# Moving the weights' tiles to multiples of 256 bytes, and 512-wide activation sets in a pool of their own, in a two-layer decoder trunk

## The chip, the cores and the metric

The kernel runs on one core of a Trainium2 chip. The metric is device time in microseconds (us), the median of three runs. A core has five engines with their own instruction queues: TensorE (PE, with its weight loads listed apart as PEld), VectorE (DVE), ScalarE (ACT), GpSimd (POOL) and SyncE (SP), which here only issues DMAs. All work on tiles in the on-chip memory SBUF, which has 128 partitions. In this document a tile's **place** is the byte at which it begins within its partition.

## The reference, cut to what matters

A sequence of 512 tokens, with 16 learned meta tokens ahead of it (528 columns in all), passes two layers of width 1024. Both layers end in the same kind of MLP:

```
mix = even_mixer(hn, ...) if layer % 2 == 0 else odd_mixer(hn, ...)
h = h + mix
h = h + sq_relu_mlp(rmsnorm(h, norm_mlp_g[layer]), mlp_w1[layer], mlp_w2[layer])

def sq_relu_mlp(h, w1, w2):
    return jnp.square(jax.nn.relu(h @ w1)) @ w2        # 1024 -> 4096 -> 1024
```

Layer 0 mixes by a retention and a convolution (weights `w_in`, `w_out`), layer 1 by stick-breaking attention (`w_qkv`, `w_o`). The meta tokens are dropped at the end, so the last products of layer 1 (its output projection and its MLP) are needed for 512 columns alone, while everything before works on 528. All of it is float32.

## The kernel before, in words

Features lie on the partitions, tokens along them. The weights come in 219 blocks of 128 output columns (`raw`, 4 KB in each partition), in the order of use. Each block is split into a high and a low float32r part, `whi` and `wlo`, of the same size. Pool `wp` holds two `raw`, three `whi` and three `wlo`; one part of 128 input features is 512 bytes of each.

Activations are split in the same manner into sets of eight pairs (`new_set`): for each 128 input features a high tile and a low tile. `products` forms, for one such part k, three products, each on the array with the part's 128x128 weights loaded for it: high weights by high activations (the rows `...h,whi` of a profile), high by low (`...l,whi`), low by high (`...h,wlo`). The weights are the operand that is loaded, the activations the operand that streams. Where there are 528 columns, each product is two of 264, one for each half. A call of `gemm` runs the eight parts, 48 products of 264 columns or 24 of 512. The loads of weights are instructions of their own; each is begun while the product before it streams.

By line L282 go 8448 products: 6528 of 264 columns (layer 0, and layer 1's keys and values) and 1920 of 512 (layer 1's queries 192, its output projection 192, its MLP 1536).

The MLP goes by four quarters of the 4096 hidden features. A quarter's hidden activations are a set `hid`; quarters 0 and 2 take one group of places, 1 and 3 another. In layer 1, quarters 0 and 2 take the places in pool `act` (tag "B") where the attention's output lay before, 1 and 3 those of pool `mlp1` (tag "C"). The input set of that MLP, `x3`, is in pool `actA`.

Pools are laid one behind the other, so a tile that grows moves all that lies behind it. Sets are made of tiles T = 528 columns wide, 2112 bytes, which is 64 more than a multiple of 256; eight pairs run through the remainders 0, 64, 128, 192. What a set's tile begins with is thus the same in every other part: even k has its high tile at remainder 0 and its low one at 64, odd k at 128 and 192. The second half of 264 columns lies 1056 bytes on, 32 more than a multiple of 256.

Layer 0's mixer and the attention have an order written out by hand (`Between`, `manual_schedule`), the MLPs follow the order of the code.

Of the kernel before, what the change touches and what calls it, by code (L numbers as in the profile page):

```python
# [17 lines left out]
P = 128  # L18
# [12 lines left out]
# Layer 0. What a tap of the convolution counts against DVE's share of a step, and how much of the share may pile up  # L31
TAP, CAP = 0.70, 1.5
# per head, the steps from one chunk of the retention to the next
WAIT = (2, 5, 3, 1)
# steps before the two sums of the layer norm
LW = (3, 1)
# per head, the steps from a chunk of the next head's retention to the turning back of this one
AGE = (2, 3, 1, 1)
# the block of w_in after which the input carries the tokens' norm
RN = 6  # L40
# products of zeros at the start; parts by which the second block lags; the part after which the norm is taken
WARM, LAG, RK = 10, 2, 0
# the pieces in which a block of the weights is split during layer 0's mixer and the attention
CUTS = 4
# Layer 1, in steps from the start of a head's work: scores of a block of queries (Z), turning of a
# block of keys (T), products with the values (V), end of a head (E), turning of the meta keys (M)
ZS, TS, VS = (0, 1, 1, 3), (10, 10, 10, 13), (16, 18)
ES, MS = (23, 30), 20
# steps before the norm of the keys, its Newton step, a pair's heads, the turning of the values
# [11 lines left out]
# columns of the parameter block  # L61
# [10 lines left out]
# columns of the constant block: what depends on shapes alone  # L72
# [15 lines left out]
# pairs of heads whose part of w_o is added while the last heads are still at work  # L88
# [3 lines left out]
def unit_order():  # L92
    """The 128-column blocks of the weights, in the order in which they are used."""
    units = []
    for j in range(NK):
        units += [("w_in", 0, 4096 + j * P), ("w_in", 0, 3072 + j * P)]
    for h in range(RH + 1):
        if h < RH:
            units += [("w_in", 0, 512 + h * P), ("w_in", 0, h * P)]
            units += [("w_in", 0, 1024 + h * 256 + e * P) for e in range(2)]  # L100
        if h > 0:
            units += [("w_in", 0, 2048 + (h - 1) * 256 + e * P) for e in range(2)]
    for part in range(2):
        units += [("w_out", part * D, m * P) for m in range(NK)]
    units += mlp_units(0)
    for p in range(8):
        units += [("w_qkv", 0, p * P), ("w_qkv", 0, D + p * P), ("w_qkv", 0, 2 * D + p * P)]
    units += [("w_oa", 0, m * P) for m in range(NK)]
    units += [("w_ob", KA * P, m * P) for m in range(0, NK, NK // (NK - KA))]
    units += mlp_units(1)  # L110
    return units
# [17 lines left out]
def trunk(ctx, tc, xT, wts, par, con, out):  # L129
# [14 lines left out]
    # the convolution's input: DVE's second operand from SBUF would shut out Pool, and the reverse  # L144
# [29 lines left out]
    def prepare(n=1, now=1):  # L174
        """The next block of the weights in two parts, the first `now` of n pieces at once."""
# [44 lines left out]
    class Between:  # L220
        """Work that goes between the products of a block, a step at a time.

        A chain tells after each step what it took of TensorE and of DVE; the filling
        takes what is left of DVE's share, and None ends it for this step."""
# [27 lines left out]
        def turn(self, n=1):  # L252
            """For the use of the spare banks of PSUM, n steps after the last."""
            while self.idle < n:
                yield None
            self.idle = 0
# [4 lines left out]
        def chain_up(self):  # L261
            """Everything but the filling, to its end."""
# [21 lines left out]
    def gemm(what, x, n, at=NK, each=None):  # L284
        """One 128-column block of x @ w, features on partitions: 3 float32r products."""
# [19 lines left out]
    def new_set(pl, tag, name):  # L305
        return [
            (pl.tile([P, T], F32R, tag=f"{tag}h{k}", name=f"{name}h{k}"),
             pl.tile([P, T], F32R, tag=f"{tag}l{k}", name=f"{name}l{k}"))
            for k in range(NK)
        ]  # L310
# [11 lines left out]
    class Sum:  # L322
# [12 lines left out]
        def total(self, dst, scale, bias=0.0, banks=None):  # L335
            """dst = scale * sum + bias on every partition."""
# [25 lines left out]
    def rsqrt(dst, xv, shape, name, pl=None, tag="rs"):  # L362
        """dst = xv ** -0.5: the table's value and a Newton step."""
# [5 lines left out]
    def rstd(sums, name, scaled=False, pl=None, tag="rb", banks=None):  # L369
        n = sums.n  # L370
        xv = sp.tile([P, T], F32, tag="xv", name=f"{name}xv", bufs=1)
# [8 lines left out]
    def residual(what, x, n, norm=None, xset=None, name="", keep=True):  # L380
        """h += x @ w, and what the next norm and product need of h."""
# [26 lines left out]
    oz = cp.tile([P, 2], F32, name="oz")  # L408
# [4 lines left out]
    # TensorE's clock opens after some work: products of zeros until the data is there  # L413
# [18 lines left out]
    # the first two blocks follow the arrival of h, the second LAG parts behind  # L432
# [37 lines left out]
    # convolution: ACT starts two sums, DVE adds the other taps to them in turn  # L470
# [36 lines left out]
    def conv_all():  # L507
# [8 lines left out]
        # layer norm  # L516
# [16 lines left out]
        xv = sp.tile([P, T], F32, tag="xv", name="lnxv", bufs=1)  # L533
# [51 lines left out]
    def normal(k):  # L585
        """The normalised input, in places that are free yet."""
# [9 lines left out]
    def renorm(k):  # L596
        """After block RN the input carries the tokens' norm."""
        nc.scalar.copy(setA[k][0], ys[k])
        if k:
            renorm_low(k - 1)  # L600
# [10 lines left out]
    # the third block, in the banks that are free yet  # L611
# [50 lines left out]
    def retention(hd, kr, qr, vt):  # L662
# [7 lines left out]
        for c in range(len(CH) + 1):  # L670
            yield from between.turn()
            if c < len(CH):
                c0, n = CH[c]
                cs = slice(c0, c0 + n)
                # tokens on partitions
# [5 lines left out]
                # scores, decayed  # L681
# [31 lines left out]
        # group norm  # L713
# [26 lines left out]
    def gated(hd, e, g):  # L740
        """Back to features on partitions, gate."""
# [48 lines left out]
    def mlp(layer, x, s, n, mine, after):  # L790
        rb = None
        with tc.tile_pool(name=f"mlp{layer}", bufs=1, reuse_waits="tile") as pl, tc.tile_pool(name=f"mlpt{layer}", bufs=2, reuse_waits="tile") as pt2:
            hid = {}
            res = None
            for which, c in MLP_STEPS:
                if which == 1:
                    hid[c] = new_set(*(mine if c % 2 == 0 else (pl, "C")), f"hid{layer}{c}")
# [39 lines left out]
    # products of what the nearer keys left; column 0 stays 1  # L837
    Eb = [ap1.tile([P, T - P * q], F32, name=f"E{q}") for q in range(NQ)]
    # meta keys of a pair of heads: 16 columns each at 0 and 64, again at 32 and 96, zero between
# [5 lines left out]
    # their transpose, per head the high part on 32 partitions and the low part on the next 32  # L845
# [37 lines left out]
    def queries(p):  # L883
        """A pair of heads in two parts, and what the scales of the scores need, tokens on partitions."""
# [32 lines left out]
    def keys(p, qxv):  # L917
        """An RMS-normalised pair of heads in two parts; the token's own norm cancels."""
# [12 lines left out]
        def chain():  # L931
# [27 lines left out]
            # the two parts of a head on the two halves of the partitions  # L959
# [11 lines left out]
    def values(p):  # L971
        """Tokens on partitions, high and low part side by side."""
# [33 lines left out]
    def attend(p, vs):  # L1006
# [8 lines left out]
        def Z(a, q):  # L1015
            """Stick-breaking weights of a head and a block of queries, keys nearest first."""
# [31 lines left out]
        def turn(a, kb):  # L1048
            """Keys on partitions."""
# [41 lines left out]
    def token_norm():  # L1091
        """The token norm, features and tokens on partitions."""
# [10 lines left out]
    def done(k):  # L1103
        """The place of setE's k-th part goes to the attention's output."""
# [21 lines left out]
    setF = new_set(actA, "A", "x3")  # L1126
# [18 lines left out]
    mlp(1, setF, s, SEQ, (act, "B"), after1)  # L1145
# [77 lines left out]
```

## Time and profile before

| | |
|---|---|
| median of three runs | 1414.18 us (1413.68 to 1415.06) |
| span of the profiled execution | 1411.5 us |
| TensorE busy | 1391.4 us, 99% of the span |
| VectorE busy | 877.5 us, 62% |
| ScalarE busy | 606.6 us, 43% |
| GpSimd busy | 357.8 us, 25% |
| DMA, share of 16 engines | 30.3% |

The span runs from the first to the last instruction; the profile gives no total for the profiled execution beside it. The timed runs are 2.2 to 3.6 us longer than this span, which is the start and end around it. A matmul's record in the profile is longer than the step from its start to the next one's, because matmuls overlap in the array and their ends are modelled; the record's length still shifts with the step.

### The profile page before, as it was taken

To read this page: it belongs to the slowest core of one execution; us is meant where nothing else is said; L and a number is where in the kernel's file an instruction comes from. 1 tells how busy PE (TensorE), PEld (TensorE's weight loads), DVE (VectorE), ACT (ScalarE), POOL (GpSimd) and SP (SyncE) were. 2 spreads that over 40 slices of the span, in tenths; PEclk is the share of its full clock that TensorE was granted. 3 is DMA by queue.
4 is the path that set the end of the run, shared out by engine and by line. 5 is a ranking of instruction groups with operands and counts; after the bars stand their busy time and mean duration, and the time that the engine had idled before them with its cause. 6 is when DMAs were issued, how large, how long until landed. Compare 5 with 4: busy or idle time off the path is not lost.

```text
span 1411.5 us, 23379 instructions
## 1 busy us (share of the span) xinstructions
PE 1391.4 (99%) x9396; PEld 1278.0 (91%) x9396; DVE 877.5 (62%) x1461; ACT 606.6 (43%) x1136; POOL 357.8 (25%) x414
## 2 busy tenths in 40 slices
PE   8999999999999999999999999998999999999998
PEld 7999999999999999999999889997878888888887
DVE  5998999966344434334345899999985433434332
ACT  6434545567443313223132677776454322323220
POOL 2656455355500000000016433335640000000000
PEclk9999999999999999999999999999999999999999
DMA  5332121123223222332233434333323332232332
GB/s 200 92 94 87 61 76 61 61 75 105 91 90 90 90 90 91 90 90 91 90 91 89 143 98 134 98 101 91 90 90 104 96 99 90 100 94 91 104 97 82
DMA packets 39643, 134.00 MB, mean 95 GB/s; under 512 B 4976, under 2 KB 5104, under 8 KB 39536
## 3 DMA queue, kind: packets, MB, share of 16 engines
q1 hardware_dynamic: 39536, 132.52, 30.3%
q8 instruction: 74, 1.21, 0.4%
q14 instruction: 33, 0.27, 0.1%
HBM read 117.69 MB, written 2.10 MB: 85 GB/s over the span
## 4 chain that ended last, share of the span: by engine, by line
PE 93%; DVE 4%; issue 1%; ACT 1%; POOL 0%; DMA 0%; POOLq 0%; SPq 0%; ACTq 0%; DVEq 0%
PE mm L282 72%; PE qk L282 11%; PE pz L1031 2%; PE po L1063 1%; PE pw L1053 1%; PE po L693 1%; DVE mT L1074 1%; PE po L697 1%; PE po L695 0%; DVE acc L489 0%; PE pk L936 0%; PE pv L679 0%; PE pt L751 0%; PE pq L899 0%; DMA h<-xT 0%
## 5 line engine op out<-in xcount | busy, mean ns | idle before, releaser
L193 ACT CAST whi<-raw 128x256 fp32r<-128x256 f32 (+1 forms) x338 | 212.0, 659 | 501.0 <-PE mm L282 461.9
L194 POOL TENSOR_TENSOR wlo<-raw,whi 128x256 fp32r<-128x256 f32 (+1 forms) x334 | 280.2, 857 | 285.6 <-ACT whi L193 136.1
L194 DVE TENSOR_TENSOR wlo<-raw,whi 128x1024 fp32r<-128x1024 f32 (+1 forms) x134 | 165.3, 1234 | 21.9 <-ACT whi L193 14.8
L385 DVE TENSOR_TENSOR h<-mm,h 128x528 f32<-128x528 f32 (+1 forms) x64 | 44.9, 701 | 214.1 <-PE mm L282 214.1
L489 DVE SCALAR_TENSOR_TENSOR acc<-cx,ptm,acc 128x526 f32<-128x526 f32 (+28 forms) x232 | 157.6, 740 | 3.5 <-ACT cx L484 3.5
L282 PE MATMUL mm<-xnh,whi 128*128 128x264 f32 x640 | 136.0, 294 | 0.0
L282 PE MATMUL mm<-xnl,whi 128*128 128x264 f32 x640 | 130.7, 286 | 2.4 <-DVE xnl L318 2.2
L282 PE MATMUL mm<-xnh,wlo 128*128 128x264 f32 x640 | 130.9, 286 | 0.0
L282 PE MATMUL mm<-x1h,whi 128*128 128x264 f32 x512 | 104.8, 286 | 0.0
L282 PE MATMUL mm<-x1h,wlo 128*128 128x264 f32 x512 | 104.3, 285 | 0.0
L282 PEld LDWEIGHTS mm<-xnh,whi 128*128 128x128 f32 x640 | 101.7, 191 | 2.8 <-issue 1.3
L282 PE MATMUL mm<-x1l,whi 128*128 128x264 f32 x512 | 103.7, 284 | 0.0
L282 PEld LDWEIGHTS mm<-xnl,whi 128*128 128x128 f32 x640 | 99.6, 190 | 3.2 <-DVE xnl L318 2.5
L282 PE MATMUL mm<-x3h,wlo 128*128 128x512 f32 x256 | 101.8, 398 | 0.0
L282 PE MATMUL mm<-x3l,whi 128*128 128x512 f32 x256 | 100.3, 392 | 0.5 <-DVE x3l L318 0.5
L282 PE MATMUL mm<-x3h,whi 128*128 128x512 f32 x256 | 100.3, 392 | 0.0
L282 PEld LDWEIGHTS mm<-xnh,wlo 128*128 128x128 f32 x640 | 100.0, 189 | 0.1
L332 POOL TENSOR_TENSOR n2s<-n2q,n2q 128x528 f32<-128x528 f32 x1 | 1.9, 1869 | 339.3 <-ACT n2q L351 339.3
L282 PE MATMUL qk<-x2h,whi 128*128 128x264 f32 (+1 forms) x320 | 82.9, 323 | 0.4 <-ACT kraw L923 0.4
L805 DVE SCALAR_TENSOR_TENSOR r<-mm,m0rb 128x528 f32<-128x528 f32 x32 | 22.7, 708 | 96.3 <-PE mm L282 96.2
L282 PEld LDWEIGHTS mm<-x1h,whi 128*128 128x128 f32 x512 | 80.2, 189 | 0.1
L282 PEld LDWEIGHTS mm<-x1h,wlo 128*128 128x128 f32 x512 | 79.8, 188 | 0.0
(400 smaller groups left out, 3343.3 us busy)
## 6 DMA issues: line engine op xcount, KB each, us to landing
raw<-wts SPq DMA_DIRECT2D x217, 512.0 KB, 3.5
Q<-qhl SPq DMA_DIRECT2D x32, 256.0 KB, 4.5
K<-khl SPq DMA_DIRECT2D x32, 132.0 KB, 3.6
h<-xT SPq DMA_DIRECT2D x8, 264.0 KB, 5.9
out<-h SPq DMA_DIRECT2D x8, 256.0 KB, 2.0
ctm<-con SPq DMA_DIRECT2D x1, 790.0 KB, 7.0
raw<-wts SPq DMA_DIRECT2D x2, 256.0 KB, 3.7
ca<-con SPq DMA_DIRECT2D x1, 256.0 KB, 6.0
```

The costliest lines, as they stand in the source:

```text
L193: copy(hi[:, ks], raw[:, ks])
L194: eng.tensor_tensor(lo[:, ks], raw[:, ks], hi[:, ks].bitcast(F32), ALU.subtract)
L282: nc.tensor.matmul(p, a[:, k, :], b[:, sl], start=(first and t == 0), stop=(last and t == 2))
L385: nc.vector.tensor_tensor(v2(h[m][:, :n], n), ps, v2(h[m][:, :n], n), ALU.add)
L489: nc.vector.scalar_tensor_tensor(a, cxf[:, s:T], tap(j, s), a, ALU.mult, ALU.add)
L693: nc.tensor.matmul(po[:n, :256], st[:n, :n], vk[:n], start=True, stop=Pst is None)
L697: nc.tensor.matmul(po[:, 256:], kt[:n], vk[:n], start=True, stop=True)
L805: nc.vector.scalar_tensor_tensor(v2(r, n), ps, 0.0, v2(rb[:, :n], n), ALU.max, ALU.mult)
L1031: nc.tensor.matmul(pz[:, :w], Q2[a][:, t, q * P:(q + 1) * P], K2[a][:, k0:k0 + w], start=(t == 0), stop=(t == 1 and i > 0))
L1053: nc.tensor.transpose(px[:, q * P:(q + 1) * P], Ws[a, q][:, (kb - q) * P:(kb - q + 1) * P], ident)
L1063: nc.tensor.matmul(po[a][:, :KQ[kb]], vs[:, kb, a], wt[kb], start=(kb == 3 and t == 0), stop=False)
L1074: nc.vector.tensor_tensor(mT[lo], pm[lo], mT[lo].bitcast(F32), ALU.subtract)
```

## The change

It has two parts. `oz`, a tile of 2 columns, becomes one of 50, of which the same two are used, and the tile `xv` gets 16 columns that nothing uses. This moves what lies behind them. And `new_set` takes a width: in layer 1's MLP the sets are 512 columns wide, 2048 bytes, and quarters 0 and 2 get places in the pool `mlp1` (tag "D") and no longer those of the attention's output.

```
+XV = T + 16
...
-    def new_set(pl, tag, name):
+    def new_set(pl, tag, name, n=T):
         return [
-            (pl.tile([P, T], F32R, tag=f"{tag}h{k}", name=f"{name}h{k}"),
-             pl.tile([P, T], F32R, tag=f"{tag}l{k}", name=f"{name}l{k}"))
+            (pl.tile([P, n], F32R, tag=f"{tag}h{k}", name=f"{name}h{k}"),
+             pl.tile([P, n], F32R, tag=f"{tag}l{k}", name=f"{name}l{k}"))
...
-        xv = sp.tile([P, T], F32, tag="xv", name=f"{name}xv", bufs=1)
+        xv = sp.tile([P, XV], F32, tag="xv", name=f"{name}xv", bufs=1)[:, :T]
...
-    oz = cp.tile([P, 2], F32, name="oz")
+    oz = cp.tile([P, 50], F32, name="oz")
...
-                    hid[c] = new_set(*(mine if c % 2 == 0 else (pl, "C")), f"hid{layer}{c}")
+                    hid[c] = new_set(*((mine or (pl, "D")) if c % 2 == 0 else (pl, "C")), f"hid{layer}{c}", n)
...
-    setF = new_set(actA, "A", "x3")
+    setF = new_set(actA, "A", "x3", SEQ)
...
-    mlp(1, setF, s, SEQ, (act, "B"), after1)
+    mlp(1, setF, s, SEQ, None, after1)
```

The places that result, as the two built programs have them (the remainder is by 256):

| tiles | first place before, remainder | first place after, remainder |
|---|---|---|
| `raw`, `whi`, `wlo` | 19264, 64 | 19456, 0 |
| sums in `sp` | 52032, 64 and 128 | 52224, 0 and 64 |
| `xv` | 56256, 192 | 56448, 128 |
| sets of layer 0, of the attention's input and output | 0, 64, 128, 192 in turn | the same remainders |
| attention's own tiles (`Q2`, `K2`, `vs`, `wTh`, ...) | | the same remainders |
| `x3` | 117504; 0, 64, 128, 192 in turn | 117760; all 0 |
| `hid10`, `hid12` | 83712; 0, 64, 128, 192 in turn | 150528; all 0 |
| `hid11`, `hid13` | 151296; 0, 64, 128, 192 in turn | 183296; all 0 |

No instruction is added, removed or moved: the two programs have the same instructions in the same order on all five engines (6371 different rows on TensorE, 1433 on VectorE, 1026 on ScalarE, 184 on GpSimd, 272 on SyncE), and each waits for the same semaphores. Only addresses differ. The comments are gone as well, so line numbers of the changed kernel are three or so higher.

## Rows read from the trace of the kernel before

**Rows 1.** The page: span, and busy time by engine.

```profile
span 1411.5 us, 23379 instructions
...
PE 1391.4 (99%) x9396; PEld 1278.0 (91%) x9396; DVE 877.5 (62%) x1461; ACT 606.6 (43%) x1136; POOL 357.8 (25%) x414
```

**Rows 2.** The page: chain that ended last, by engine and by line.

```profile
PE 93%; DVE 4%; issue 1%; ACT 1%; POOL 0%; DMA 0%; POOLq 0%; SPq 0%; ACTq 0%; DVEq 0%
...
PE mm L282 72%; PE qk L282 11%; PE pz L1031 2%; PE po L1063 1%; PE pw L1053 1%; PE po L693 1%; DVE mT L1074 1%; PE po L697 1%; PE po L695 0%; DVE acc L489 0%; PE pk L936 0%; PE pv L679 0%; PE pt L751 0%; PE pq L899 0%; DMA h<-xT 0%
```

**Rows 3.** Waits of TensorE: us in total, times, longest.

```profile
PE pz L1031 <- DVE wTl L1056: 6.2, 1, 6.2
PE mm L282 <- DVE xnl L318: 2.2, 1, 2.2
```

**Rows 4.** Waits of the DMA queue on SyncE; DMA issues by us to landing.

```profile
SPq L166 <- DVE wlo L194: 655.9, 128, 11.1
SPq L166 <- POOL wlo L194: 532.0, 84, 14.8
...
raw<-wts SPq DMA_DIRECT2D x217, 512.0 KB, 3.5
```

**Rows 5.** Stretches of layer 0's MLP and layer 1's MLP, busy us by engine.

```profile
core 0: us, PE busy (x) PEld busy (x) DVE busy (x) ACT busy (x) POOL busy (x), PEclk, DMA share, GB/s
...
391.60:761.00 369.40, 369.40 (x3024) 369.40 (x3024) 149.43 (x175) 109.63 (x141) 17.49 (x23) 1.00 0.29 90
1058.46:1411.50 353.04, 349.43 (x1512) 283.34 (x1511) 140.15 (x160) 98.92 (x127) 0.00 (x0) 1.00 0.30 96
```

**Rows 6.** The chain in order of time, two pieces: start us, us, what.

```profile
391.60 369.58 PE mm L282 x3024
...
1058.46 349.44 PE mm L282 x1512
```

**Rows 7.** Products of one even part, 264 wide (500.20 to 500.68): busy us, mean ns.

```profile
L282 PE MATMUL mm<-hid00h,whi 128*128 128x264 f32 x2 | 0.4, 288 | 0.0
L282 PE MATMUL mm<-hid00l,whi 128*128 128x264 f32 x2 | 0.4, 288 | 0.0
L282 PE MATMUL mm<-hid00h,wlo 128*128 128x264 f32 x2 | 0.4, 286 | 0.0
```

**Rows 8.** Products of the odd part after it (500.90 to 501.41).

```profile
L282 PE MATMUL mm<-hid00h,wlo 128*128 128x264 f32 x2 | 0.4, 285 | 0.0
L282 PE MATMUL mm<-hid00h,whi 128*128 128x264 f32 x2 | 0.4, 284 | 0.0
L282 PE MATMUL mm<-hid00l,whi 128*128 128x264 f32 x2 | 0.4, 280 | 0.0
```

**Rows 9.** Products of one even part, 512 wide (1199.95 to 1200.41).

```profile
L282 PE MATMUL mm<-x3h,wlo 128*128 128x512 f32 x1 | 0.4, 397 | 0.0
L282 PE MATMUL mm<-x3l,whi 128*128 128x512 f32 x1 | 0.4, 392 | 0.0
L282 PE MATMUL mm<-x3h,whi 128*128 128x512 f32 x1 | 0.4, 389 | 0.0
```

**Rows 10.** Products of the odd part after it (1200.62 to 1201.10).

```profile
L282 PE MATMUL mm<-x3h,wlo 128*128 128x512 f32 x1 | 0.4, 399 | 0.0
L282 PE MATMUL mm<-x3h,whi 128*128 128x512 f32 x1 | 0.4, 391 | 0.0
L282 PE MATMUL mm<-x3l,whi 128*128 128x512 f32 x1 | 0.4, 391 | 0.0
```

**Rows 11.** Attention's 512-wide products by L1063, both tiles at remainder 0, weights at 96.

```profile
L1063 PE MATMUL po<-wTh,vs 128*128 128x512 f32 x16 | 6.4, 398 | 0.0
...
L1063 PE MATMUL po<-wTl,vs 128*128 128x512 f32 x16 | 6.3, 395 | 0.0
```

More of the change, by code (lines that the diff above doesn't have):

```diff
@@ L532, in conv_all @@
         yield from wait(LW[1])
-        xv = sp.tile([P, T], F32, tag="xv", name="lnxv", bufs=1)
+        xv = sp.tile([P, XV], F32, tag="xv", name="lnxv", bufs=1)[:, :T]
         s.total(xv, 1.0 / D, EPS, "cx")
```

## The prediction, made before the changed kernel had run

> **What bounds the kernel now.** I read the page first: TensorE is busy for 1391.4 of 1411.5 us [rows 1]. The chain that ended last says the same from the other side, 93% of it is TensorE, 72% and 11% of it the products of L282 [rows 2]. The waits then tell whether anything holds TensorE up: the longest is 6.2 us, once, in the attention, and the next 2.2 us at the start [rows 3]. The weights' DMAs wait for free buffers, hundreds of microseconds in all, and land 3.5 us after issue; TensorE never waits for them [rows 4]. In the two MLPs TensorE is busy without a gap, save 3.6 us after the very last product, while VectorE is busy for 149.43 of 369.40 us and 140.15 of 353.04 [rows 5]. So in these two stretches, half of the span, the time is the number of products times the step from one to the next, and nothing else.
>
> That step is the number to look at. 3024 products of 264 columns follow each other in 369.58 us, 122.2 ns each, and 1512 of 512 columns in 349.44 us, 231.1 ns each [rows 6]. The granted clock in both stretches is 1.00 [rows 5], which is the 2.4 GHz level; 264 cycles of it are 110.0 ns and 512 are 213.3, so each step holds some 12 or 18 ns beyond a cycle for each column. Products of one shape, on the same engine at the same clock and with nothing to wait for, are not equally long: 280 to 288 ns at 264 columns [rows 7, 8], 389 to 399 at 512 [rows 9, 10]. They differ in nothing but which tiles they read. So places do enter the step, by some nanoseconds, and this change touches nothing else.
>
> **The change part by part.** No instruction, order or wait changes. The padding of `oz` and `xv` costs no time; no instruction reads it. The new places of quarters 0 and 2 free them from the attention's output tiles, but TensorE waits for nothing in that stretch [rows 3, 5], so nothing is gained by it. `raw` moves with the weights; if its transfers or its splits became faster or slower, that stays hidden: the DMAs wait for buffers anyway [rows 4], and VectorE has over 200 us of slack in each MLP [rows 5]. Were that cover gone, it would show as TensorE waiting for `wlo`. What is left is the step of the 8448 products.
>
> I describe a product by the distance of its streaming tile from the weights' place, by 256. Before, the weights are at 64. An even part has the high tile at distance 192 (both of its products) and the low one at 0, an odd part the high one at 64 and the low one at 128. The second halves lie 32 on, in the mean of each row. After, the weights are at 0, and where the sets keep their width, even parts are at 0, 64, 0, odd parts at 128, 192, 128: each distance moves up by 64.
>
> *264 columns, 6528 products.* Rows by distance: 0 is 288; 128 is 280; 64 is 284 and 285; 192 is 288 and 286 [rows 7, 8]. Before, six rows sum to 862 + 849 = 1711. After, with the mean price at each distance, 288 + 284.5 + 288 + 280 + 287 + 280 = 1707.5. That is 3.5 ns less in six, 0.58 ns a product, times 6528 is 3.8 us. But two slots at one distance differ by up to 2 ns, as much as the whole effect, so the distance does not tell everything (what streams before and after enters too). With such an error of 1.5 ns a product the bounds are 2.1 ns gained (13.6 us) and 0.9 ns lost (6.0 us). I take half of the mean, **-1.9 us**.
>
> *512 columns in layer 1's MLP, 1536 products.* All now stand at distance 0. The mean of the six rows is (389 + 392 + 397 + 391 + 391 + 399) / 6 = 393.2; the one row at distance 0, the low tile of the even part, is 392 [rows 9, 10]. The bounds are the shortest row, 389, which gains 4.2 ns or 6.5 us, and the longest, 399, which loses 5.8 ns or 8.9 us. I take the row at the same distance: 1.2 ns less, **-1.9 us**.
>
> *512 columns, queries and output projection, 384 products.* Their sets keep their width. By the same exchange, with rows 9 and 10, (392 + 395 + 392) + (391 + 393 + 391) = 2354 in place of 2359, 0.8 ns a product, **-0.3 us**.
>
> The sum is -1.9 - 1.9 - 0.3 = -4.1 us: a span of 1407.4 in place of 1411.5. The runs lie 2.7 us above the span in their median, so the time is 1414.2 - 4.1 = **1410.1 us**, 0.3% faster. A measurement of this kernel can tell some 0.2%, 2.8 us, from no change.
>
> **The rivals.**
>
> *Nothing happens.* In a stream without gaps both operands run through every remainder by 256 within one product (512 bytes of weights, 1056 or 2048 of activations), so wherever they meet, they may meet equally often; a shift of all distances then only permutes long and short products. For it: the even and odd parts, 862 and 849, differ by only 1.5%, and their order would simply be changed. Against it: with the sets at one remainder nothing is left to average in layer 1. The time is 1414.2, within 2 us.
>
> One rule of the Trainium skill speaks for this rival. The page "TensorE: Matmul & The Clock Gate", section "Part 2: What happens when you issue a matmul", says that TensorE has two independent read ports and that loading the next tile's weights does not steal read bandwidth from the running matmul. Taken as it stands, places could not matter, and the sum would be 0. The trace does not bear it out fully: 280 and 288 ns for products that differ only in places [rows 7, 8].
>
> *Everything runs clean.* If it is at other remainders alone that the two reads disturb each other, every product of layer 1's MLP comes out at the shortest row, 389 ns, and gains 4.2 ns: 6.5 us. With the full exchange at 264 columns, 3.8 us, the time is 1414.2 - 10.3 = 1403.9. For it speaks that one row in six stands there already; against it that the row at distance 0 is not the shortest.
>
> *Slower: operands that begin at one place collide.* In layer 1's MLP each product now begins at the remainder at which its weights begin and at which the product before it began and ended. The only rows in which a 512-wide product follows one of its own remainder are those of the attention, 398 and 395 [rows 11], at distance 160. Their mean, 396.5, is 3.3 ns over 393.2; over 1536 products that is 5.1 us, 1419.3 if the 264-wide ones give nothing. It decides when it costs more than 1.4 ns a product beyond today's mean, since the other terms give 2.2 us. Against it: in L1063 the weights come from another tile, at another distance, and the row at distance 0 in layer 1's own stream is below the mean and not above.
>
> **How the numbers follow.** I give the forecast 0.45 (its own range 1406 to 1414; of it 0.27 beyond 2.8 us, 0.17 within, 0.01 slower). Nothing happens: 0.22 (0.18 within, 0.02 on either side). Clean: 0.16, all faster. Collision: 0.17 (0.14 slower, 0.03 within). Together 0.45 faster, 0.38 within 0.2%, 0.17 slower. The range takes in the clean case nearly whole and the collision up to its price from rows 11: 1403 to 1419, which leaves out the deeper gain at 264 columns and a loss at 399.
>
> **What would show it.** The two long pieces of the chain give each term alone: x3024 from 369.58 us to about 368.7, x1512 from 349.44 to about 347.6. In the rows of one part, the 264-wide even part should read 288, 284, 288 and the odd one 280, 287, 280 in the order of the code; in layer 1 all three rows of x3 should be equal or nearly so, at 392, in even and odd parts alike. The first term is wrong if the even part stays longer by its old rows, the second if the three rows settle near 389 or near 397. Any wait of TensorE beyond those of rows 3 would mean that the argument by steps misses something.

## Result and profile after

The changed kernel takes 1400.19 us (median of four runs, 1398.76 to 1400.36) beside 1413.93 us for the kernel before in the same series (1411.90 to 1415.06): a ratio of 0.9903, with a 95% interval of 0.9891 to 0.9915. The forecast was 1410.1 us with a range of 1403 to 1419. The direction was right; the gain of 13.7 us is over three times the 4.1 us forecast, and the time lies below the range. Each run whose span is on record takes 1.7 to 1.9 us longer than that span, which is the start and end around it; the 2.2 to 3.6 us given above for the kernel before also hold the difference between its executions. One run of e12 in ten, 1932.7 us at a granted clock of 0.65, is left out of that kernel's median.

The page of the changed kernel, span and busy time by engine, as in [rows 1]:

```profile
span 1398.3 us, 23379 instructions
...
PE 1377.2 (98%) x9396; PEld 1270.3 (91%) x9396; DVE 878.2 (63%) x1461; ACT 606.3 (43%) x1136; POOL 358.0 (26%) x414
```

The span is 13.2 us shorter, TensorE is busy for 14.2 us less, and the other engines are busy as before. The two long pieces of the chain, start, length and count, answer to [rows 6]:

```profile
389.92 364.58 PE mm L284 x3024
...
1051.82 342.85 PE mm L284 x1512
```

The same 3024 products take 5.00 us less (120.6 ns each, 122.2 before), and the same 1512 take 6.59 us less (226.8 ns, 231.1 before). The first piece starts 1.68 us earlier, which is what layer 0's mixer gave in this pair of traces (the start of that piece scatters by 2 us between kernels whose layer 0 is alike, as is seen below). From the end of the first piece to the start of the second, the attention, it is 297.32 us, and 297.28 in [rows 6] (297.2 to 298.0 in all runs); behind the second piece it is 3.6 us in both. So 1.68 + 5.00 + 6.59 = 13.3 us is the whole gain of 13.2.

The stretches of layer 0's MLP, the attention and layer 1's MLP, in the columns of [rows 5]:

```profile
389.92:754.50 364.58, 364.58 (x3025) 364.58 (x3025) 149.39 (x175) 109.56 (x141) 17.55 (x23) 1.00 0.29 91
754.50:1051.82 297.32, 285.27 (x1855) 251.10 (x1855) 278.32 (x608) 197.22 (x428) 134.30 (x137) 0.99 0.37 105
1051.82:1398.30 346.48, 342.83 (x1512) 283.36 (x1511) 140.09 (x160) 98.78 (x127) 0.00 (x0) 1.00 0.30 98
```

TensorE is busy without a gap in both MLPs again, at a granted clock of 1.00, with VectorE at work for 149 and 140 us as before. In the attention VectorE is busy for 278.32 of 297.32 us: there it is not TensorE alone that sets the time. TensorE's waits, total, times and longest, are those of [rows 3] with a few tenths more or less:

```profile
PE pz L1034 <- DVE wTl L1059: 6.3, 1, 6.3
PE mm L284 <- DVE xnl L320: 2.7, 1, 2.7
```

No wait of note has gone and none has come, so in the two MLPs the whole difference is in the step from product to product. It is not a matter of what other engines do meanwhile: in the changed kernel, from 1062.65 us to the end, every block of 24 products takes 226.6 or 226.7 ns a step in the mean, while VectorE is at work for only two fifths of the stretch and idle for the rest. In layer 1's MLP (1059.82 to 1391.82 us, products of `x3`) the rows, busy us and mean ns of one, answer to [rows 9, 10]:

```profile
L284 PE MATMUL mm<-x3l,whi 128*128 128x512 f32 x237 | 92.2, 389 | 0.0
L284 PE MATMUL mm<-x3h,wlo 128*128 128x512 f32 x237 | 92.2, 389 | 0.0
L284 PE MATMUL mm<-x3h,whi 128*128 128x512 f32 x236 | 91.8, 389 | 0.0
```

All three are equal, as forecast, but at 389 ns, the shortest of the six rows before, and not at the 392 ns of the row at distance 0. In layer 0, one odd part (500.60 to 501.10 us), answering to [rows 8]:

```profile
L284 PE MATMUL mm<-hid00h,whi 128*128 128x264 f32 x2 | 0.4, 286 | 0.0
L284 PE MATMUL mm<-hid00l,whi 128*128 128x264 f32 x2 | 0.4, 282 | 0.0
L284 PE MATMUL mm<-hid00h,wlo 128*128 128x264 f32 x2 | 0.4, 282 | 0.0
```

And the even part after it (501.35 to 501.85 us), answering to [rows 7]:

```profile
L284 PE MATMUL mm<-hid00h,whi 128*128 128x264 f32 x2 | 0.4, 284 | 0.0
L284 PE MATMUL mm<-hid00l,whi 128*128 128x264 f32 x2 | 0.4, 283 | 0.0
L284 PE MATMUL mm<-hid00h,wlo 128*128 128x264 f32 x2 | 0.4, 282 | 0.0
```

Forecast were 280, 287, 280 and 288, 284, 288. The odd part is no shorter than before (850 beside 849); the even part has lost 13 ns (849 beside 862). The long even part has come down to the odd one, instead of the two changing places.

### The profile page after: what moved, and what is told of

Its sections match the earlier page's. It is cut to its first block, busy times and chain, and to the rows that moved or that the text cites. A ratio compares the mean times of both kernels' runs of the same rounds, so it can differ in the third digit from the quotient of the medians.

```text
span 1398.3 us, 23379 instructions
## 1 busy us (share of the span) xinstructions
PE 1377.2 (98%) x9396; PEld 1270.3 (91%) x9396; DVE 878.2 (63%) x1461; ACT 606.3 (43%) x1136; POOL 358.0 (26%) x414
## 4 chain that ended last, share of the span: by engine, by line
PE 91%; DVE 6%; issue 1%; ACT 1%; POOL 0%; DMA 0%; POOLq 0%; SPq 0%; ACTq 0%; DVEq 0%
PE mm L284 72%; PE qk L284 10%; PE pz L1034 1%; PE po L1066 1%; DVE E L1043 1%; PE pw L1056 1%; PE po L696 1%; DVE mT L1077 1%; PE po L700 1%; PE po L698 0%; DVE acc L492 0%; DVE hdn L595 0%; DMA h<-xT 0%; PE pv L682 0%; PE pt L754 0%
## 5 line engine op out<-in xcount | busy, mean ns | idle before, releaser
L284 PEld LDWEIGHTS mm<-x1l,whi 128*128 128x128 f32 x512 | 79.5, 188 | 0.0
```

The source lines that it names most:

```text
L284: nc.tensor.matmul(p, a[:, k, :], b[:, sl], start=(first and t == 0), stop=(last and t == 2))
```

## Experiments

All places below are remainders by 256. The distance of a product is the place of its stream less that of the weights. A step is from the start of one product to the start of the next in the trace. Steps of one set are means over its products in the piece x1512, from start to start; weighted by their counts they give that piece's length. The record of a product in the rows is 160 to 164 ns longer than its step, and not by the same amount in every slot. Some expectations below quote steps that are up to 0.7 ns off such means: 228.7 for what is 229.0 at distance 64, 231.7 for 232.4 at 128, 233.7 for 233.3 at 32, and 234.0 for 234.3 at 160. That places count by 256 is seen in the kernel before: from one part to the next but one, the streams of layer 1's MLP move by 7424 bytes against their weights, 29 times 256, and each slot's step in `hid10` to `hid13` comes back to within 0.2 ns. The kernels:

| kernel | weights | `x3`; `hid10`,`12`; `hid11`,`13` | median us | x3024 us | x1512 us |
|---|---|---|---|---|---|
| before | 64 | 0, 64, 128, 192 in turn | 1413.93 | 369.58 | 349.44 |
| changed | 0 | all 0 | 1400.19 | 364.58 | 342.85 |
| e1 | 0 | in turn | 1405.58 | 364.58 | 349.47 |
| e2 | 64 | all 0 | 1417.44 | 369.58 | 352.80 |
| e3 | 64 | all 64 | 1398.99 | 364.56 | 342.85 |
| e4 | 0 | 64; 128; 192 | 1405.27 | 364.58 | 349.18 |
| e5 | 0 | 32; 96; 160 | 1409.47 | 364.58 | 353.16 |
| e6, `hid01`,`03` at 0 | 0 | all 0 | 1399.87 | 364.15 | 342.85 |
| e7, as e6, halves 256 + 272 | 0 | all 0 | 1398.88 | 364.46 | 342.86 |
| e8 | 0 | 224; 128; 16 | 1407.99 | 364.57 | 351.97 |
| e9 | high 0, low 128 | all 0 | 1407.94 | 366.25 | 349.48 |
| e10 | 128 | all 0 | 1408.35 | 364.58 | 352.81 |
| e11 | 192 | all 0 | 1412.42 | 371.28 | 346.15 |
| e12 | high 0, low 64 | `x3`, `hid10`,`12`: high 0, low 64; `hid11`,`13`: 0 | 1412.54 | 368.75 | 350.27 |

In e3 layer 0's sets move by 64 with the rest, so all its relations are those of the changed kernel. The kernel before took 1413.3 to 1414.1 us beside the others.

**The weights alone** (e1). Edit against the kernel before:

```diff
-    oz = cp.tile([P, 2], F32, name="oz")
+    oz = cp.tile([P, 50], F32, name="oz")
...
-        xv = sp.tile([P, T], F32, tag="xv", name=f"{name}xv", bufs=1)
+        xv = sp.tile([P, T + 16], F32, tag="xv", name=f"{name}xv", bufs=1)[:, :T]
```

> Only the weights' places move (to multiples of 256 bytes); the sets of layer 1's MLP stand as before, at 0, 64, 128 and 192 in turn. Two theories. DISTANCE: a product's length follows from how far its streaming tile lies from the weights, by 256; then all four distances still occur equally often in layer 1's MLP, the piece x1512 of the chain stays at 349.4 us, and only the 264-wide part gains (the mixer 1.7 us, the piece x3024 from 369.6 to 364.6): 1413.9 - 6.7 = 1407.2 us. SUCCESSION: what counts is whether a product's stream goes on at the remainder at which the product before it ended, the weights' place matters less; then layer 1's MLP still jumps between remainders as before and may move by some ns a product either way, with x1512 between 346 and 350 us: 1404 to 1408 us. ALIGNMENT of the weights (a tile that begins at a multiple of 256 loads quicker, whatever streams): x1512 comes down to about 343 and the time to about 1401 us with the weights alone.

Measured 1405.58 us, a ratio of 0.9943 (0.9927 to 0.9960). The chain's two pieces:

```profile
388.28 364.58 PE mm L282 x3024
...
1050.77 349.47 PE mm L282 x1512
```

The whole gain of layer 0's MLP is there, to 0.01 us, so it comes from the place of the weights and from nothing in the new sets. Layer 1's MLP takes what it took before, as the theory by distance says: all four distances still occur equally often. Succession allowed this too (346 to 350 us). That weights gain by beginning at a multiple of 256 as such is refuted for this stretch.

**The sets alone** (e2). Edit against the kernel before: the change without the two lines above, that is

```diff
-    def new_set(pl, tag, name):
+    def new_set(pl, tag, name, n=T):
...
-    mlp(1, setF, s, SEQ, (act, "B"), after1)
+    mlp(1, setF, s, SEQ, None, after1)
```

> Only the sets of layer 1's MLP change (512 wide, all at remainder 0); the weights stay at 64, so every product of that stretch streams at distance 192 from them. All theories: the piece x3024 stays at 369.6 us, as the weights and layer 0's sets stand as before. DISTANCE: the two rows of before at distance 192 are 397 and 389 ns, mean 393, as the mean of all six; x1512 stays at about 349 us and the time at about 1413.9. ALIGNMENT: the same. SUCCESSION: all streams at one remainder, no jump from product to product, so every product takes 227 ns as with the whole change; x1512 is about 343 us and the time 1413.9 - 6.6 = 1407.3 us.

Measured 1417.44 us, slower than before: 1.0029 (1.0019 to 1.0038). The pieces:

```profile
392.50 369.58 PE mm L282 x3024
...
1060.10 352.80 PE mm L282 x1512
```

The new sets, with nothing else, cost 3.4 us in layer 1's MLP. They differ from the changed kernel in the weights' place alone, and that is worth 9.95 us there. Succession is refuted: all streams are at one remainder, and the mean step is longer than before, 233.3 ns where it was 231.1. Distance had it that these sets would not gain, but put the step at 231 ns, the mean of the mixture. The parts of the change do not add up: -7.9 and +3.9 us against -13.7 together, all measured beside the kernel before.

The 233.3 ns is a mean. Two parts of `x3` in a row (from 1200.80 and from 1201.50 us):

```profile
L282 PE MATMUL mm<-x3l,whi 128*128 128x512 f32 x1 | 0.4, 398 | 0.0
L282 PE MATMUL mm<-x3h,whi 128*128 128x512 f32 x1 | 0.4, 393 | 0.0
L282 PE MATMUL mm<-x3h,wlo 128*128 128x512 f32 x1 | 0.4, 393 | 0.0
```

```profile
L282 PE MATMUL mm<-x3h,whi 128*128 128x512 f32 x1 | 0.4, 398 | 0.0
L282 PE MATMUL mm<-x3h,wlo 128*128 128x512 f32 x1 | 0.4, 398 | 0.0
L282 PE MATMUL mm<-x3l,whi 128*128 128x512 f32 x1 | 0.4, 393 | 0.0
```

Every second product is long, whichever it is: the steps alternate between 230 or 231 ns and 235 or 236, though all products stand at the same places by 256. So the step of a single product is not set by its places alone; what they set is at most the mean of a repeating pattern.

**Everything 64 bytes on** (e3), against the changed kernel:

```diff
-    oz = cp.tile([P, 50], F32, name="oz")
+    oz = cp.tile([P, 66], F32, name="oz")
```

> The whole change, and everything 64 bytes further on: weights and layer 1's sets all at remainder 64, every distance and every succession as in the changed kernel, only nothing begins at a multiple of 256 any more. DISTANCE and SUCCESSION: no change from the changed kernel, x3024 364.6, x1512 342.9, 1400.2 us. ALIGNMENT: the gain goes back, x3024 near 369.6 and x1512 near 349.4, 1412 to 1414 us.

Measured 1398.99 us (0.9895, 0.9880 to 0.9910), with both pieces within 0.02 us of the changed kernel's. No tile that counts begins at a multiple of 256 here. Alignment is refuted: a common shift by 64 bytes changes nothing, so what counts is how the places lie to each other.

**Other places for the sets** (e4, and later e5 and e8). The edit lets each set begin further on; the numbers are those of e4, in columns of 4 bytes:

```diff
-    def new_set(pl, tag, name, n=T):
+    def new_set(pl, tag, name, n=T, pad=0):
+        def tile(t, k):
+            e = pad if (t, k) == ("h", 0) else 0
+            return pl.tile([P, e + n], F32R, tag=f"{tag}{t}{k}", name=f"{name}{t}{k}")[:, e:]
+        return [(tile("h", k), tile("l", k)) for k in range(NK)]
...
-    setF = new_set(actA, "A", "x3", SEQ)
+    setF = new_set(actA, "A", "x3", SEQ, 16)
```

> The whole change, with the weights at 0, but layer 1's sets at other remainders, all tiles of a set alike: x3 at 64, hid10 and hid12 at 128, hid11 and hid13 at 192. Three distances are tried in one run, x3 being half of the products and the others a quarter each. SUCCESSION: only the first product of a set follows a jump, so all stay at 227 ns a step; x1512 342.9 us, 1400.2 us. DISTANCE, priced by the rows of before at 64 (399, 391), 128 (391) and 192 (397, 389) against 389 for the cleanest: 6, 2 and 4 ns more, in the mean 4.5 ns over 1512 products, 6.8 us: x1512 349.7 us, 1407 us.

Measured 1405.27 us (0.9938, 0.9923 to 0.9953). Rows of the sets at 64 and at 192, layer 1's MLP from 1058.70 to 1390.70 us:

```profile
L284 PE MATMUL mm<-x3h,wlo 128*128 128x512 f32 x237 | 93.3, 393 | 0.0
L284 PE MATMUL mm<-x3l,whi 128*128 128x512 f32 x237 | 92.7, 391 | 0.0
L284 PE MATMUL mm<-x3h,whi 128*128 128x512 f32 x236 | 92.0, 390 | 0.0
L284 PE MATMUL mm<-hid11h,wlo 128*128 128x512 f32 x64 | 25.3, 396 | 0.0
L284 PE MATMUL mm<-hid11l,whi 128*128 128x512 f32 x64 | 25.3, 395 | 0.0
```

x1512 is 349.18 us where distance, priced by old rows, gave 349.7, and succession 342.9. By steps, with a whole set at one distance: 226.7 ns at 0 (the changed kernel), 229.0 at 64, 232.4 at 128, 233.3 at 192. Their mean is 230.4, and the mixture before ran at 231.1: it had been a mean over good and bad places, with 0.7 ns more on top.

> The whole change, weights at 0, layer 1's sets at other remainders, all tiles of a set alike: x3 at 32, hid10 and hid12 at 96, hid11 and hid13 at 160. The runs so far gave, for a 512-wide product whose stream stands d behind the weights: 226.7 ns a step at d = 0, 228.7 at 64, 231.7 at 128, 233.3 at 192. DISTANCE, smooth: between these, 227.7 at 32, 230.2 at 96, 232.5 at 160, in the mean 229.5 over 1512 products: x1512 347.0 us, 1404.4 us. DISTANCE, but in places of 64 bytes: a stream that begins in the middle of such a place meets two of them, and all three sets come out at the worse of their neighbours or beyond, 229, 232, 233 or more: x1512 349 us or more, 1406 us or more.

Measured 1409.47 us (0.9970, 0.9960 to 0.9979), x1512 353.16 us, the worst of all. A set at 32 takes 233.3 ns, at 96 233.3, at 160 234.3. The smooth theory is refuted: 32 bytes off the best place cost more than 64 do.

**Low weights elsewhere** (e9), against the changed kernel; the gaps hold the rest of the tiles at their remainders:

```diff
+        if not ready:
+            wp.tile([P, 32], F32, tag="gap", name="gap", bufs=1)
         lo = wp.tile([P, NK, P], F32R, tag="wlo", name=f"wlo{u}", bufs=3)
+        if not ready and u == 0:
+            wp.tile([P, 32], F32, tag="gap2", name="gap2", bufs=1)
```

> The whole change, but the low parts of the weights 128 bytes further on, high parts and all streams as in the changed kernel. In layer 1's MLP two products of three have their own weights at distance 0, the third (high tile by wlo) at 128. While a product streams, TensorE loads the weights of the next one. OWN weights count: the step of the product by wlo goes from 226 to some 232 ns, the other two stay at 227. NEXT weights count (the load running beneath the stream): the step of the product ahead of it, low tile by whi, whose successor takes wlo, goes to some 232 ns, and that of wlo itself stays at 226. Either way the mean is 228.4 ns, x1512 345.3 us; for the 264-wide products the mixed distances of the wlo slots are exchanged, within 1 us or so of 364.6; 1402 to 1404 us. If the weights' place did not count: 1400.2 us.

What the expectation rests on is seen in the changed kernel's timeline (start us, length, what), first the products and then the weight loads:

```profile
1200.01 0.39 PE L284 MATMUL mm<-x3h,whi 128*128 128x512 f32 x1
1200.24 0.39 PE L284 MATMUL mm<-x3l,whi 128*128 128x512 f32 x1
```

```profile
1200.01 0.19 PEld L284 LDWEIGHTS mm<-x3l,whi 128*128 128x128 f32 x1
1200.24 0.19 PEld L284 LDWEIGHTS mm<-x3h,wlo 128*128 128x128 f32 x1
```

The load for the next product starts within 0.01 us of the stream's own start and runs beneath it for 188 ns of the 227. Measured 1407.94 us (0.9964, 0.9951 to 0.9977); rows of e9, 1061.04 to 1393.04 us:

```profile
L288 PE MATMUL mm<-x3h,wlo 128*128 128x512 f32 x237 | 94.1, 397 | 0.0
L288 PE MATMUL mm<-x3l,whi 128*128 128x512 f32 x237 | 93.9, 396 | 0.0
L288 PE MATMUL mm<-x3h,whi 128*128 128x512 f32 x236 | 91.8, 389 | 0.0
```

The low tile by `whi` has its own weights at distance 0 and still goes from 389 to 396 (232.5 ns a step): what runs beneath it is the load of `wlo`, at distance 128, where whole sets took 232.4 to 233.3. That fits the theory of the next weights. But the product by `wlo` is slow as well (234.1 ns), though the load beneath it stands at 0. So own weights alone don't give the step, and the load beneath doesn't alone; that it is part of the cause fits these rows but is not shown. x1512 came out 4.2 us above what either theory said. Moving one tile in three undid the whole gain of the stretch (349.48, before 349.44).

**Low parts of both sides at 64** (e12), against the changed kernel: as e9 with gaps of 16 and 48, and `x3`, `hid10`, `hid12` with

```diff
+    def new_set(pl, tag, name, n=T, low=0):
+        def tile(t, k):
+            e = low if t == "l" else 0
+            return pl.tile([P, n + 4 * e], F32R, tag=f"{tag}{t}{k}", name=f"{name}{t}{k}")[:, e:e + n]
...
+    setF = new_set(actA, "A", "x3", SEQ, 16)
```

> The whole change, with the low parts of the weights at 64 instead of 0, and in x3, hid10 and hid12 the low tiles at 64 as well; high parts of both at 0; hid11 and hid13 all at 0. The order of the products is high by high weights, low by high weights, high by low weights, and the weights loaded beneath a stream are those of the next product: high, then low, then high. So in x3, hid10, hid12 every stream stands where the load beneath it stands (0 over 0, 64 over 64, 0 over 0), though both jump from product to product, while by its own weights the low tile stands at 64 and the product by low weights at 192. LOAD BENEATH THE STREAM: these sets run at 226.7 ns a step as in the changed kernel. OWN weights: 0, 64, 192, that is 226.7, 228.7, 233.3, mean 229.6. Jumps cost by themselves: 230 to 232. In hid11 and hid13 the stream stays at 0 and only the loads jump, as in the run with the low weights at 128 (231.2 ns there): 228 to 231 in every theory. x1512: 343.5 us by the first, 347 by the second, 348 to 350 by the third. The 264-wide products get another mixture, 362 to 370 us for x3024. Time: 1399 to 1403 us by the first, 1402 to 1410 by the others.

Measured 1412.54 us (0.9991, 0.9981 to 1.0000), x1512 350.27 us: nearest to the third theory. Rows of e12, 1067.08 to 1399.08 us:

```profile
L288 PE MATMUL mm<-x3h,wlo 128*128 128x512 f32 x237 | 93.8, 396 | 0.0
L288 PE MATMUL mm<-x3l,whi 128*128 128x512 f32 x237 | 93.2, 393 | 0.0
L288 PE MATMUL mm<-x3h,whi 128*128 128x512 f32 x236 | 92.7, 393 | 0.0
L288 PE MATMUL mm<-hid10h,wlo 128*128 128x512 f32 x64 | 25.4, 398 | 0.0
...
L288 PE MATMUL mm<-hid12h,whi 128*128 128x512 f32 x64 | 25.3, 395 | 0.0
...
L288 PE MATMUL mm<-hid10h,whi 128*128 128x512 f32 x64 | 25.1, 392 | 0.0
...
L288 PE MATMUL mm<-hid12h,wlo 128*128 128x512 f32 x64 | 25.0, 391 | 0.0
```

With the load beneath each stream at distance 0, but both jumping, `x3` takes 231.9 ns. So the distance to the load beneath is not all either. That the jump of stream or weights from product to product has a price of its own would explain it, but the rows of `hid10` and `hid12` warn against pricing single products: quarters 0 and 2 lie in the same bytes and meet weights at the same places, and yet the product by `wlo` is the longest in one (398) and the shortest in the other (391), at 232.2 and 231.1 ns a step in the mean. `x3` itself runs at 232.2 ns before `hid11` comes and at 231.1 after it. What came before thus enters: a stream can fall into one of several patterns and keep it.

**Weights at 128 and 192** (e10, e11), against the changed kernel; e10 is shown, e11 has 34 and 32:

```diff
-XV = T + 16
+XV = T + 48
...
-    oz = cp.tile([P, 50], F32, name="oz")
+    oz = cp.tile([P, 18], F32, name="oz")
```

> The whole change, but the weights at remainder 128 instead of 0; all sets stand as in the changed kernel, layer 1's MLP streams at remainder 0, that is at distance 128. DISTANCE at 512 columns: 231.7 ns a step, as hid10 and hid12 had with streams at 128 and weights at 0; x1512 350.3 us. At 264 columns, DISTANCE alone, priced by the mean step of all slots before and after at each distance (0: 119.7, 32: 124.3, 64: 122.3, 96: 121, 128: 119, 160: 120.3, 192: 123, 224: 122 ns): 121.2 ns in the mean, x3024 366.6 us. That price had slots at one distance that differ by 7 ns, so it may be off by 2 ns a product, 6 us. Time by both: about 1411 us.

> The same with the weights at 192, so that layer 1's MLP streams at distance 64. DISTANCE at 512 columns: 228.7 ns a step, x1512 345.8 us. At 264 columns, priced as in the run with weights at 128: 121.7 ns, x3024 367.9 us. Time by both about 1408 us. If the 264-wide products go instead by which slots follow which, none of the four places of the weights need rank as priced: 362 to 370 us.

Measured 1408.35 us (0.9960, 0.9946 to 0.9975) and 1412.42 us (0.9993, 0.9984 to 1.0003). e10:

```profile
388.17 364.58 PE mm L284 x3024
...
1050.23 352.81 PE mm L284 x1512
```

e11:

```profile
393.61 371.28 PE mm L284 x3024
...
1062.46 346.15 PE mm L284 x1512
```

At 512 columns distance 64 takes 228.9 ns (346.15 / 1512), now with the streams at 0, and 229.0 in e4; distance 128 takes 233.3, and 232.4 in e4: equal distances, not quite equal steps. At 264 columns the price by distance missed both, by 2.0 and 3.4 us. Weights at 128 give 364.58 us like weights at 0, for a plain reason that I overlooked: the sets stand at 0 and 64 in even parts and at 128 and 192 in odd ones, so 128 bytes only exchange the parts. Weights at 64 and 192 should be alike by the same reason, but are 369.58 and 371.28. Before, the steps of layer 0's MLP repeat after 12 products (two parts), in e11 only after 24: again another pattern at like places. Why is open.

**Finer places** (e8), with the edit of e4, and for `hid11`, `hid13` each tile 64 columns longer and begun at its fifth:

> The whole change, weights at 0, layer 1's sets at other remainders: x3 at 224, hid10 and hid12 at 128, hid11 and hid13 at 16, all tiles of a set alike. So far: 226.7 ns at distance 0, 228.7 at 64, 231.7 at 128, 233.3 at 192, but 233.7 at 32, 233.3 at 96 and 234.0 at 160. PLACES OF 64 BYTES: what stands off a multiple of 64 takes 233 to 234 ns, so x3 at 224 and hid11, hid13 at 16 alike; hid10, hid12 231.7 as before; mean 233.1, x1512 352.5 us, 1409.5 us. PLACES OF 32 BYTES: 16 bytes off might cost less than 32, and 224, the nearest to 0 from below, could be cheap: any of the two at 227 to 229 would show it; x1512 345 to 350 us.

Measured 1407.99 us (0.9957, 0.9940 to 0.9973), x1512 351.97 us. `x3` at 224 takes 233.3 ns; `hid11` and `hid13` at 16 take 231.7, so 16 bytes already cost 5.0 ns over a set at 0, and 224 costs 6.6. `hid12` at 128 takes 232.4, as in e4, and `hid10`, in the same bytes and the same run, 233.3: a stream can settle in either. The time, 1407.99 us, is near the 1409.5 of places of 64 bytes; no set came out at 227 to 229.

**Layer 0's sets in line** (e6), against the changed kernel, and e7, which also cuts the halves at 256 columns:

```diff
+            (pl.tile([P, n + pad], F32R, tag=f"{tag}h{k}", name=f"{name}h{k}"),
+             pl.tile([P, n + pad], F32R, tag=f"{tag}l{k}", name=f"{name}l{k}"))
...
+                    hid[c] = new_set(*((mine or (pl, "D")) if c % 2 == 0 else (pl, "C")), f"hid{layer}{c}", n, 48 if layer == 0 and c % 2 else 0)
...
+            halves = [(slice(0, 256), ps[:, 0, 256:]), (slice(256, T), ps[:, 1, :T - 256])]
```

> The whole change, and the tiles of hid01 and hid03 (layer 0, 264 columns by half) 2304 bytes apart, so that all of them begin at remainder 0: first halves at distance 0 from the weights, second halves at 32. 768 of the 3024 products of the piece x3024 read them; today these take 120.6 ns a step in the mean, 117 to 123. DISTANCE: uniform and near 0, these steps come down to 117 to 119 ns; x3024 from 364.6 to 362 to 363.4 us, 1397.5 to 1399 us. If what counts at 264 columns is something else (second halves that begin 32 bytes on), the steps settle anywhere from 120 to 123: x3024 364 to 366.5, 1400 to 1402 us.

> As the run before, and the halves of layer 0's MLP are 256 and 272 columns instead of 264 and 264, so that second halves begin at the remainder of the first: hid01 and hid03 then stand at distance 0 throughout, x1, hid00 and hid02 at 0, 64, 128, 192 in turn, both halves alike. In sum the columns are the same. DISTANCE: hid01 and hid03 take the least of all, at most 117 to 119 ns in the mean of the two halves; the others 119 to 122, as a mean over all distances; x3024 361 to 364 us, 1397 to 1400 us. If the halves' 32 bytes did not matter: no difference from the run before by over 1 us.

Measured 1399.87 us (0.9906, 0.9891 to 0.9921) and 1398.88 us (0.9901, 0.9886 to 0.9916), x3024 364.15 and 364.46 us. The 768 products of e6 gained 0.6 ns each, 0.43 us in all where distance had 1.2 to 2.6; their steps settled at 120.0 ns, in the second case of the expectation. In e7, where both halves of `hid01` and `hid03` stand at distance 0, their step is 122.0 ns, while the sets at 0, 64, 128, 192 in turn come down from 120.6 to 120.0. The expectation by distance had it the other way, `hid01` and `hid03` the shortest. So what is worth 4.4 ns at 512 columns does not carry over to these narrower products: with all at one place they were the slowest of their stretch. Neither kernel, nor e3, can be told from the changed one by its time; none beats it.

## Why the prediction was wrong

**What bounds the kernel** was right: the time of both MLPs is the count of products times the step, no wait entered, and the two pieces of the chain carry 11.6 of the 13.2 us. That places enter the step was right too. The Trainium skill, "TensorE: Matmul & The Clock Gate", section "Part 2: What happens when you issue a matmul", has it that loading the next tile's weights does not steal read bandwidth from the running matmul. The traces do not bear it out for these products: with the same streams, x1512 takes 352.80 us with the weights at 64 and 342.85 with them at 0 (e2 and the changed kernel).

**The step that failed at 512 columns**: "I take the row at the same distance: 1.2 ns less". It measured 4.4 ns, -6.6 us where -1.9 were forecast (1.2 ns times 1536 is 1.8). The row at distance 0 [rows 9] stood in a mixture, and there a product's own distance does not set its step: in e9 a product at distance 0 from its own weights goes from 389 to 396 ns when only its neighbour's weights move. So 392 was the price of distance 0 among unlike neighbours, and not that of a stream in which all stand alike. It was also the length of a record. By starts, that product steps 231.6 ns in `hid10` to `hid13`, above the mean of 231.1, so that the same reasoning on steps would have forecast no gain at all. The bound that I had put beside it, the shortest row, 389 ns and 6.5 us, was the answer. So the rival "everything runs clean" had this term right, and what I held against it, that the row at distance 0 was not the shortest, was this same misreading.

**The step that failed at 264 columns**: "I take half of the mean". The exchange by distance gave 0.58 ns a product, half of it 0.29; the long piece measured 1.65. Not the halving alone was wrong: even the full 0.58 is a third of what came, and e10 and e11 show that a price by distance misses the piece by 2.0 and 3.4 us. What was right is the text's own doubt, "the distance does not tell everything", and the bound of 2.1 ns. In the mixer, 2688 of these products stand, and 1.68 us is 0.6 ns for each. This is all that is known of it: the nine kernels whose weights stand to layer 0's sets as in the changed one or 128 off, high and low alike, start the long piece at 388.2 to 390.1 us, those at 64 or 192 at 391.6 to 393.6.

**The third term**, -0.3 us for queries and output projection, cannot be seen (297.32 beside 297.28 us, where all runs scatter by 0.8), and 768 of the 6528 products counted at 264 columns stand in the same attention stretch. I counted products in a stretch in which VectorE is busy for 94% of the time and stands in the chain, so that the step alone does not set its end.

**The other rivals.** "Nothing happens" fell with the result. "Operands that begin at one place collide" is wrong for this place (342.85), but a slower outcome of the same kind was near: the same sets over weights at 64 are slower than before (e2). The forecast priced the two halves of the change only together; measured, 9.7 of the 13.7 us come from doing both.

**The range** left out the depth. The two terms' own bounds reached 20 us of gain together and held the result; the range stopped at the clean case, 1403, priced with 0.58 ns for the 264-wide products.

**What stays open** is the rule for one slot. Shown is that the place of streams and weights relative to each other sets the mean step of whole sets at 512 columns, to about 1 ns (e1 to e5), and that a single product's step also hangs on its neighbours (e9) and on what ran before (e2, e8, e12). That the load beneath a stream is the cause is argued from e9 and not shown. Why equal distances can settle at 232.4 or 233.3 ns, why weights at 64 and 192 differ at 264 columns, why a common place is no gain there (e7), and why the best place leaves 13 ns over 512 cycles (226.7 beside 213.3 ns) was not found.

## What to carry to other kernels

Where TensorE runs without a gap and each product loads new weights, look at the places of streams and weights by 256. For products of 512 columns, give all streams and all weights of a stage one common remainder, and do it for both sides or not at all, since one side alone was worth +3.4 or 0 us where both were worth -6.6. For narrower products measure first: halves of 256 and 272 columns at one common place took 122.0 ns a step, mixed ones 120.0. Rows taken from a mixture of places don't price a uniform one, because a row carries its neighbours, and a record's length is not the step; bound such a change by the shortest and the longest row and keep that range. Count products only where the step sets the end, and not in stretches in which another engine is busy for 94% of the time.

## What the runs showed of the hardware

- The step of a 512-wide product of float32r at a granted clock of 1.00, with a weight load beneath each, is 226.7 to 234.3 ns in the mean of a set, by the place of the stream relative to the weights: 226.7 at 0, 231.7 at 16 bytes, 233.3 at 32, 229.0 at 64, 233.3 at 96, 232.4 or 233.3 at 128, 234.3 at 160, 233.3 at 192 and 224.
- The steps of single products alternate even where all places are alike by 256 (231 and 236 ns in e2, 229 and 238 in e10), and tiles in the same bytes can run in two patterns in one execution (`hid10` and `hid12` in e12, 232.2 and 231.1 ns).
- A common shift doesn't matter: 64 bytes more on everything left both pieces within 0.02 us (e3).
- One operand in three out of line costs as much as all four places mixed: 349.48 us with `wlo` moved by 128 bytes, 349.44 before.
- At 264 columns the effect is smaller, and not of one sign: sets with their first halves at the weights' place gained 0.6 ns a product (e6), and with both halves there they were 2.0 ns slower than the mixed sets beside them (e7). The weights' place alone moves the long piece by up to 6.7 us (364.58 to 371.28).
